# Low halves of weights by accumulating DMAs in more stages, additions on VectorE, and reordered heads, in a two-block transformer kernel

## The chip, the cores and the metric

The kernel runs as one program on one core of a Trainium2 chip. The metric is the device time of one execution in microseconds (us). Before the change three executions took 1567.94, 1572.04 and 1572.07 us, median 1572.04. The execution that was profiled took 1570.88 us, of which the trace covers a span of 1569.1 us.

Names of engines: PE is TensorE (PEld its weight load), DVE is VectorE, ACT is ScalarE, POOL is GpSimd, SP issues plain DMAs. "L174" is line 174 of the kernel before.

## The reference

512 tokens of width 1024 pass through two blocks, all in float32. Cut to what matters:

```python
def first_block(x, mem, ...):                       # one layer
    h = rmsnorm(x, g_mix_pre)
    aq, ak, av, iq, ik, iw, bq, bk, bv, cq, gate_logits = split(h @ w_in)
    mkv = rmsnorm(mem, g_mem) @ w_mem_kv
    ya = dsa_attention(aq, ak, av, iq, ik, iw, rel_bias) @ w_up_a   # top-k keys by an index score
    yb = stick_breaking_attention(bq, bk, bv) @ w_up_b
    yc = memory_attention(cq, mk, mv) @ w_up_c
    merged = gates[0] * ya + gates[1] * yb + gates[2] * yc
    x = x + rmsnorm(merged @ w_out, g_mix_post)
    gu = rmsnorm(x, g_ffn_pre) @ w_ffn_in
    x = x + rmsnorm((silu(gu[:F]) * gu[F:]) @ w_ffn_out, g_ffn_post)

def second_block(x, p, ...):
    h = h + mlstm_layer(h)       # conv + silu on q, k; gates i, f; per head: decay matrix, values, norm, o, z
    h = ple_add(h, p[0])         # h + (p @ w_proj) * sigmoid(rms_norm(h) @ w_gate)
    k, v = shared_kv(h)          # rotary keys
    h = h + dilated_layer(h, k, v)   # three dilations, softmax over them, silu(z) gate, w_out
    h = ple_add(h, p[1])

# stick breaking, per head, with z = q k^T / 8 and a strictly causal mask:
log_beta = log_sigmoid(z)
tail = reverse_cumsum(log_sigmoid(-z)) - log_sigmoid(-z)
a = exp(log_beta + tail);  out = a @ v
```

## The kernel before, in words

**Every product is three products.** TensorE multiplies values rounded to a short float32 form, so both operands are kept as a rounded high half and a low half that holds the rest, and a product is high·high + low·high + high·low. A block of weights of 128 x 1024 (512 KB) gives 24 matmuls of 512 columns, called a unit below.

**Weights are prepared just ahead of their use.** `pre` (L150) takes the next block in the order of use: SP loads it into one of two buffers `wraw`, the high half `wh` is a rounded copy (one of three buffers), the low half `wl` (one of three) is made in one of three ways. Either DVE subtracts `wraw - wh` (L174), or POOL does (L172), or, where `low_dma` is set, ACT writes `-wraw` rounded into `wl` and a DMA issued by POOL adds the same block from memory on top (L165, L166). `pool_share` chooses between L172 and L174; `low_dma` holds in the stick-breaking stage alone, where `hi_dve` also lets DVE make the high half (L160) instead of ACT (L162). Blocks scaled by a gain ("quad" and "fmg", in the dilated layer and elsewhere) go through `split` and are in none of these ways. A block is prepared as soon as a buffer comes free.

**Stages in order of the span (us):** index projections 0 to 55, memory scores and memory attention to 150, stick-breaking attention to 350, sparse attention ("dsa") to 510, up-projections and w_out to 585, first post-norm to 617, FFN to 963, second post-norm with the first projection of the mLSTM to 1004, gates ("mg") and the other q and k projections to 1039, v (token-major, two groups) and o to 1126, mLSTM heads to 1218, w_out_a to 1256, first ple 1257 to 1307, dilated layer to 1511, second ple to 1564.

**The order of work** is the order in which the code is written, with generators: a branch `yield`s after some units, and `weave` takes turns between two such generators (heads and projections that fill in between). Each engine runs its own instructions in that order, and so does POOL's queue, which issues the DMAs of L166.

**Parts that the steps below touch.** `post_norm` (L460) makes, per 128 rows of features, `t` (L469, DVE), `h + t` (DVE for the first, POOL for the others, L471 and L473), `xh` and `xl` (the split for the next stage) and the sum of squares `ss` (L304). Branch results are added to `merged` by POOL (L519). A stick-breaking head (L806) collects `z` in one PSUM buffer; ACT takes |z| (L821) and a copy of z (L823); the chain of exp, ln, max-and-add (L826), scan (L827) and subtraction (L828) then works on the copy. An mLSTM head has a broadcast `Mb` of the running maximum over partitions on POOL (L1186), a product `dg` with the identity (L1190), a broadcast `eb` (L1201), and at its end `norm` (L1235 and after). A POOL broadcast and a POOL tensor operation belong to different code libraries: the program has an instruction "ISA" without operands wherever the one follows the other. At the end of the dilated layer, `logits`, `z_tile`, `values` and `finish` run per head, and `w_out_b_2` follows.

Of the kernel before, what the change touches and what calls it, by code (L numbers as in the profile page):

```python
# [88 lines left out]
class K:  # L89
    def __init__(s, ctx, tc, A, dbg=None):  # L90
        s.ctx, s.tc, s.nc, s.A = ctx, tc, tc.nc, A
        s.dbg = dbg
        s.order = []
        s.since, s.fence, s.fenced = [], None, False
        s.ready, s.share, s.pool_share, s.hi_dve, s.low_dma = {}, 0.0, 0.0, False, False
        s.b4 = None
# [39 lines left out]
    def pre(s, *spec):  # L136

        nc = s.nc
        u = len(s.order)
        s.order.append(spec)  # L140
        raw = s.wraw.tile([128, 1024], F32, name="wraw")
        for c in ((0, 512), (512, 1024)) if u == 0 else ((0, 1024),):
            nc.sync.dma_start(raw[:, c[0]:c[1]], s.A["W"][u][:, c[0]:c[1]])
        hi = s.whp.tile([128, 1024], F32R, name="wh")
        lo = s.wlp.tile([128, 1024], F32R, name="wl")
        if u == 0:
            for c in (slice(0, 512), slice(512, 1024)):
                s.split(hi[:, c], lo[:, c], raw[:, c])
            s.ready[spec] = hi, lo
            return  # L150
        if spec[0] in ("quad", "fmg"):

            n = 2 if spec[0] == "quad" else 8
            for i in range(n):
                c = slice(1024 // n * i, 1024 // n * (i + 1))
                s.split(hi[:, c], lo[:, c], raw[:, c], s.vec(spec[-1], spec[3] * n + i))
            s.ready[spec] = hi, lo
            return
        if s.hi_dve:
            nc.vector.tensor_copy(hi, raw)  # L160
        else:
            nc.scalar.activation(hi, raw, AF.Copy)  # L162
        if s.low_dma:

            nc.scalar.activation(lo, raw, AF.Copy, scale=-1.0)  # L165
            nc.gpsimd.dma_start(lo, s.A["W"][u], accum_op=OP.add)  # L166
            s.ready[spec] = hi, lo
            return
        s.share += s.pool_share
        if s.share >= 1.0:  # L170
            s.share -= 1.0
            nc.gpsimd.tensor_tensor(lo, raw, hi.bitcast(F32), op=OP.subtract)  # L172
        else:
            nc.vector.tensor_tensor(lo, raw, hi.bitcast(F32), op=OP.subtract)  # L174
        s.ready[spec] = hi, lo
# [285 lines left out]
    def post_norm(s, r, S, g, gn):  # L461

        nc = s.nc
        s.mark("postnorm")
        bc, _ = s.rstd_from(S[0], T, 1024, cols=False)
        s.S = [None]
        for k in range(8):
            t = s.tmp.tile([128, T], F32, name="t512")
            nc.vector.scalar_tensor_tensor(t, r[:, k], s.vec(g, k), bc, op0=OP.mult, op1=OP.mult)  # L469
            if k < 1:  # L470
                nc.vector.tensor_tensor(s.h[:, k], s.h[:, k], t, op=OP.add)  # L471
            else:
                nc.gpsimd.tensor_tensor(s.h[:, k], s.h[:, k], t, op=OP.add)  # L473
            s.split(s.xs[0][:, k], s.xs[1][:, k], s.h[:, k], s.vec(gn, k))
            s.ssq_add(s.S, s.h[:, k])
# [17 lines left out]
    def up_g(s, wname, yh, yl, G, first):  # L493
# [15 lines left out]
        for j in range(4):  # L509
            for mm in range(2):  # L510
                m = 2 * j + mm
                prods(m, (3,) if m < 3 else range(4))
                ps = pss[m]
                if first:
                    nc.vector.tensor_tensor(s.merged[:, m], ps, G[:, m], op=OP.mult)
                else:
                    t = s.tmp.tile([128, T], F32, name="t512")
                    nc.vector.tensor_tensor(t, ps, G[:, m], op=OP.mult)
                    nc.gpsimd.tensor_tensor(s.merged[:, m], s.merged[:, m], t, op=OP.add)  # L519
                yield  # L520
# [39 lines left out]
    def dsa_mem(s, x, iqc):  # L560
# [5 lines left out]
        with ExitStack() as br:  # L566
# [10 lines left out]
            with ExitStack() as c:  # L577
# [15 lines left out]
                s.fm4("w_in", iqc, s.xs, ev, mid=mid)  # L593
                s.pool_share = 0.5
                ikh = one.tile([128, T], F32R, name="ikh")
# [168 lines left out]
    def stick_branch(s, br):  # L764
        nc = s.nc
        s.mark("stick")
        s.pool_share, s.hi_dve, s.low_dma = 1.0, True, True
        vp = s.pool("bv", 1, ctx=br)
# [37 lines left out]
        def logits(h):  # L806
# [14 lines left out]
            nc.scalar.activation(e, z, AF.Abs)  # L821
            c = wk.tile([128, 1280], F32, name="e")
            nc.scalar.activation(c, z, AF.Copy)  # L823
            s.act(e, e, AF.Exp, scale=-1.0)
            s.act(e, e, AF.Ln, bias=1.0)
            nc.vector.scalar_tensor_tensor(e, c, 0.0, e, op0=OP.max, op1=OP.add)  # L826
            nc.vector.tensor_tensor_scan(e[:, ::-1], keep, e[:, ::-1], 0.0, op0=OP.mult, op1=OP.add)  # L827
            nc.vector.tensor_tensor(c, c, e, op=OP.subtract)  # L828
            s.act(c, c, AF.Exp)
            st[h] = c  # L830

# [76 lines left out]
    def dsa_branch(s, br):  # L908

        nc, A = s.nc, s.A  # L910
        s.mark("dsa")
        s.pool_share, s.hi_dve, s.low_dma = 0.5, False, False
        vp = s.pool("av", 1, ctx=br)
# [103 lines left out]
        s.drain(ua[0])  # L1017
        s.pool_share = 0.0

# [69 lines left out]
    def mlstm(s):  # L1089
# [3 lines left out]
        with ExitStack() as ph:  # L1093
# [3 lines left out]
            def mid():  # L1097
                yield
                yield
                yield  # L1100
                st["bc"], st["cols"] = yield from s.rstd_g(s.S[0], T, 1024)
                s.S = [None]
# [7 lines left out]
            with ExitStack() as c3:  # L1110
# [5 lines left out]
                def conv(m, ps):  # L1116
# [3 lines left out]
                    for t in range(1, 4):  # L1120
                        nc.vector.scalar_tensor_tensor(qk[:, m], c[:, 1 + t:1 + t + T], s.vec("conv", 8 * t + m),
                                                       qk[:, m], op0=OP.mult, op1=OP.add)
                s.pool_share = 1.0
                s.fm4("w_in_a_2", [128 * m for m in range(4)], xs, conv, mid=mid)
                bc, cols = st["bc"], st["cols"]
                gp = s.pool("mg", 1, ctx=c3)
# [3 lines left out]
                def ev(ps):  # L1130
# [14 lines left out]
                    nc.vector.tensor_scalar(nM, nM, -1.0, None, op0=OP.mult)  # L1145
                s.fm(("mg",), xs, ev, m=64)
                for m in range(4, 8):
# [6 lines left out]
                for m in range(8):  # L1154
                    s.act(qk[:, m], qk[:, m], AF.Silu)
            s.pool_share = 0.0
            o = qp.tile([128, 8, T], F32, name="o")
# [16 lines left out]
            with ExitStack() as c2:  # L1174
# [83 lines left out]
                def main():  # L1258
# [4 lines left out]
                    for h in range(3):  # L1263
                        values(h)
                        weights(h + 1)
                        if h < 2:
                            decay(h + 2)
                        yield 2
                        norm(h)
                        yield 2  # L1270
                    values(3)
# [48 lines left out]
    def ple(s, l):  # L1320
        nc, A = s.nc, s.A
        s.mark("ple%d" % l)
        with ExitStack() as ph:
            pp = s.pool("ple", 1, ctx=ph)
            wk = s.pool("plew", 3, ctx=ph)
            pw = pp.tile([128, 8, T], F32, name="pw")
            nc.sync.dma_start(pw, s.pw[l])
            xs = (pp.tile([128, 8, T], F32R, name="xh"), pp.tile([128, 8, T], F32R, name="xl"))
            ks = range(8)
# [37 lines left out]
    def dilated(s):  # L1367
        nc, A = s.nc, s.A
        s.mark("dil")
        xs = s.xs  # L1370
        s.pool_share = 0.0
        with ExitStack() as ph:
# [105 lines left out]

            def keys():
                for h in range(4):  # L1480
# [6 lines left out]
            def queries(X, tiles):  # L1487
                for j, (h, g) in enumerate(tiles):
                    if g == 0:
# [113 lines left out]
            XK = rope(pk, ck)  # L1603
            X0 = qquad(0, {5: [keys]})
            X1 = qquad(1, {5: [lambda: queries(X0, QS[0])]})
            logits(0)
            z_tile(0)
            pv = quad("w_kv_2", [512 + 128 * h for h in range(4)], "norm_kv", {5: [lambda: queries(X1, QS[1])]}, False)
            for t in range(4):
                nc.scalar.activation(v[:, t], pv[t], AF.Copy, scale=cols[:, t:t + 1])  # L1610

                for c in range(4):
                    nc.sync.dma_start(vq[32 * t:32 * t + 32, c, :], v[c:128:4, t, :])
            logits(1)
            z_tile(1)
            X2 = qquad(2, {4: [lambda: values(0)]})
            z_tile(2)
            values(1)
            z_tile(3)
            for h in range(2):  # L1620
                finish(h)
            queries(X2, QS[2])
            logits(2)
            out = s.fm4_g("w_out_b_2", [128 * m for m in range(4)], xs, ev, ks=range(4))
            prods(4, range(2))
            logits(3)
            next(out)
            next(out)
            values(2)
# [11 lines left out]
            s.b4 = None  # L1641
            s.pool_share = 1.0
        if s.dbg: s.dbg("h3", s.h)
# [118 lines left out]
```

## Time and profile before

| what | value |
|---|---|
| median of three executions | 1572.04 us (1567.94 to 1572.07) |
| the profiled execution | 1570.88 us |
| its span | 1569.1 us, 17934 instructions |
| PE busy | 1511.0 us (96%), 6813 instructions |
| DVE busy | 981.8 us (63%), 1421 instructions |
| ACT busy | 721.4 us (46%), 1194 instructions |
| POOL busy | 263.5 us (17%), 165 instructions |
| mean granted clock of TensorE | 0.983 of full speed |
| low halves by DVE, by POOL, by DMA | 149, 40, 26 |

The page of the profile has the busy time of each engine, the span in 40 slices, the DMA queues, the chain of work that ended last, and the costliest groups of instructions. Other views answer for a stretch of time: what each engine waited for, the busy time in a list of windows with the granted clock, and a timeline of instructions. "Idle before <- X" is the time that an engine stood idle before an instruction and what released it; "issue" there means that nothing the trace shows was waited for.

### The profile page before, as it was taken

Reading aid. Unit: us, or ns where it says so; the run is one execution under the profiler, and the core shown is the slowest. Engines: PE = TensorE matmul, PEld = TensorE weight load, DVE = VectorE, ACT = ScalarE, POOL = GpSimd, SP = SyncE. Lnnn points to the kernel's source line nnn. Section 1 sums busy time; section 2 is a strip of 40 time slices with the busy share of each in tenths; the row PEclk is TensorE's granted clock in tenths of the full one; section 3 lists DMA queues with packets and bytes.
Section 4 is the critical chain, followed back from the end, with each engine's and each line's share of the span. In section 5 each row is a group of like instructions: output and inputs, shape, how many; then the busy total and the mean of one; then the engine's idle time right before and its main releaser. Section 6 shows DMA issues by size and latency. Waiting matters only on the chain.

```text
span 1569.1 us, 17934 instructions
## 1 busy us (share of the span) xinstructions
PE 1511.0 (96%) x6813; PEld 1237.2 (79%) x6813; DVE 981.8 (63%) x1421; ACT 721.4 (46%) x1194; POOL 263.5 (17%) x165
## 2 busy tenths in 40 slices
PE   8999999999999999999999999899999999999988
PEld 6787877778777877888888887688877778989766
DVE  6899867664776638443234335773367566886966
ACT  5544356663455446332222324353465354654543
POOL 3211110113311404110011102610022000010022
PEclk9999999999999999999999999999999999999989
DMA  5332875552222533332233333223211333223222
GB/s 191 107 102 70 176 159 133 118 131 95 91 78 74 161 105 125 101 95 94 94 96 103 97 94 127 75 81 119 83 54 55 93 135 108 81 79 96 67 93 95
DMA packets 48806, 162.01 MB, mean 103 GB/s; under 512 B 5712, under 2 KB 7120, under 8 KB 48464
## 3 DMA queue, kind: packets, MB, share of 16 engines
q1 hardware_dynamic: 44976, 147.24, 29.8%
q0 software_dynamic: 3744, 13.63, 4.9%
q8 instruction: 53, 0.87, 0.2%
q14 instruction: 33, 0.27, 0.1%
HBM read 153.50 MB, written 6.29 MB: 102 GB/s over the span
## 4 chain that ended last, share of the span: by engine, by line
PE 69%; DVE 18%; ACT 8%; issue 4%; POOL 1%; DMA 1%; SPq 0%; ACTq 0%; DVEq 0%; POOLq 0%
PE dps L128 45%; PE b L128 18%; PE z L128 3%; ACT e L122 2%; DVE ss L304 2%; DVE xl L256 1%; DVE e L827 1%; PE aps L128 1%; DVE wl L174 1%; ACT wh L162 1%; DVE aTl L253 1%; DVE score L747 1%; PE o L128 1%; DVE e L693 1%; DVE e L828 1%
## 5 line engine op out<-in xcount | busy, mean ns | idle before, releaser
L128 PE MATMUL dps<-xh,wh 128*128 128x512 f32 (+2 forms) x996 | 396.4, 398 | 5.3 <-DVE aTl L253 4.2
L162 ACT ACTIVATE wh<-wraw 128x1024 fp32r<-128x1024 f32 x189 | 199.9, 1058 | 413.3 <-PE dps L128 258.8
L128 PE MATMUL dps<-xh,wl 128*128 128x512 f32 (+2 forms) x996 | 388.3, 390 | 0.2 <-DMA wl<-in_W 0.2
L128 PE MATMUL dps<-xl,wh 128*128 128x512 f32 (+2 forms) x996 | 388.1, 390 | 0.0
L174 DVE TENSOR_TENSOR wl<-wraw,wh 128x1024 fp32r<-128x1024 f32 x149 | 188.2, 1264 | 168.9 <-ACT wh L162 163.9
L128 PEld LDWEIGHTS dps<-xh,wh 128*128 128x128 f32 (+1 forms) x996 | 187.4, 188 | 51.5 <-DVE aTl L253 6.2
L128 PEld LDWEIGHTS dps<-xh,wl 128*128 128x128 f32 (+1 forms) x996 | 187.1, 188 | 41.1 <-DMA wl<-in_W 0.7
L128 PEld LDWEIGHTS dps<-xl,wh 128*128 128x128 f32 (+1 forms) x996 | 187.5, 188 | 40.2 <-issue 1.8
L172 POOL TENSOR_TENSOR wl<-wraw,wh 128x1024 fp32r<-128x1024 f32 x40 | 102.5, 2563 | 319.8 <-ACT wh L162 295.9
L128 PE MATMUL b<-wh,xh 128*128 128x512 f32 x288 | 115.4, 401 | 0.0
L128 PE MATMUL b<-wl,xh 128*128 128x512 f32 x288 | 114.1, 396 | 0.0
L128 PE MATMUL b<-wh,xl 128*128 128x512 f32 x288 | 113.9, 396 | 0.0
L128 PE MATMUL b<-xh,wh 128*128 128x512 f32 x208 | 87.0, 418 | 7.0 <-ACT xh L252 3.9
L128 PE MATMUL b<-xl,wh 128*128 128x512 f32 x208 | 85.7, 412 | 8.3 <-DVE xl L256 7.4
L128 PE MATMUL b<-xh,wl 128*128 128x512 f32 x208 | 85.0, 409 | 3.3 <-DVE wl L174 1.8
L1044 POOL TENSOR_TENSOR g<-g,bc 128x512 f32<-128x512 f32 x22 | 38.9, 1767 | 246.8 <-ACT g L122 246.8
L128 PEld LDWEIGHTS b<-wh,xh 128*128 128x128 f32 x288 | 69.8, 242 | 7.0 <-issue 0.2
L128 PEld LDWEIGHTS b<-wl,xh 128*128 128x128 f32 x288 | 69.8, 242 | 6.6
L128 PEld LDWEIGHTS b<-wh,xl 128*128 128x128 f32 x288 | 69.7, 242 | 6.6
L128 PE MATMUL dps<-fh,wh 128*128 128x512 f32 x176 | 69.3, 394 | 0.0
L128 PE MATMUL dps<-fl,wh 128*128 128x512 f32 x176 | 69.3, 394 | 0.0
L128 PE MATMUL dps<-fh,wl 128*128 128x512 f32 x176 | 69.3, 394 | 0.0
(360 smaller groups left out, 2609.9 us busy)
## 6 DMA issues: line engine op xcount, KB each, us to landing
wraw<-in_W SPq DMA_DIRECT2D x239, 512.0 KB, 3.6
wl<-in_W POOLq DMA_DIRECT2D x26, 512.0 KB, 7.1
h<-in_x SPq DMA_DIRECT2D x16, 256.0 KB, 4.0
pw<-pwo SPq DMA_DIRECT2D x16, 256.0 KB, 2.0
pw<-pw SPq DMA_DIRECT2D x2, 2048.0 KB, 7.8
strip<-in_relb SPq DMA_DIRECT2D x8, 256.0 KB, 2.6
out<-h SPq DMA_DIRECT2D x7, 256.0 KB, 2.0
G<-in_mem SPq DMA_DIRECT2D x1, 1024.0 KB, 9.1
```

The source lines that it names most:

```text
L122: i = s.nc.scalar.activation(out, in_, func, **kw)
L128: s.nc.tensor.matmul(out, l, r, start=start, stop=stop, skip_group_check=True)
L162: nc.scalar.activation(hi, raw, AF.Copy)
L172: nc.gpsimd.tensor_tensor(lo, raw, hi.bitcast(F32), op=OP.subtract)
L174: nc.vector.tensor_tensor(lo, raw, hi.bitcast(F32), op=OP.subtract)
L253: nc.vector.tensor_tensor(lo, src, hi.bitcast(F32), op=OP.subtract)
L256: nc.vector.scalar_tensor_tensor(lo, src, scale, hi.bitcast(F32), op0=OP.mult, op1=OP.subtract)
L304: nc.vector.tensor_tensor(S[0], S[0], t, op=OP.add)
L693: nc.vector.tensor_scalar(e[:, t], e[:, t], rs[:, t:t + 1], None, op0=OP.mult)
L747: nc.vector.match_replace(w, m8, w, SENT)
L827: nc.vector.tensor_tensor_scan(e[:, ::-1], keep, e[:, ::-1], 0.0, op0=OP.mult, op1=OP.add)
L1044: nc.gpsimd.tensor_tensor(g, g, st["bc"], op=OP.mult)
```

## The change

1. **Low halves.** The subtraction on POOL (L172) is gone, and `dma_share` replaces `pool_share` and `low_dma`: where it is 1, ACT writes `-wraw` and POOL issues the accumulating DMA; where it is 0, DVE subtracts. It is 1 from the index projections on through the memory, stick-breaking and sparse stages and the up-projections that stand in them, in the mLSTM from its first projection to its end, in the first ple, from `logits(2)` of the dilated layer to the end of the kernel. The FFN, w_out and the rest of the dilated layer have 0.
2. **Additions.** The additions of L473 and L519 go from POOL to DVE.
3. **Stick breaking.** No copy of z: L826 and L828 read z in PSUM.
4. **mLSTM start.** The reciprocal norm is taken four half units into the first projection instead of three, and the gate projection's first half comes before its transposes.
5. **mLSTM heads.** The weave takes a turn between `values(h)` and `weights(h + 1)`, and one less after `norm(h)`.
6. **ple.** The tiles of the stage are placed in another order in memory, for the first ple with a gap between them.
7. **Dilated layer.** Keys and queries are turned in two halves on two hooks (5 and 6); the third query projection runs before the values' projection; at the end `logits(2)`, `values(0)`, `logits(3)`, `values(1)` come earlier, and `values(2)` and `values(3)` stand together ahead of `finish(2)` and `finish(3)`.

In counts: ACT writes 134 negative copies in place of 26 and drops 8 copies of z; POOL issues 134 accumulating DMAs in place of 26 and loses 40 subtractions and 30 additions; DVE makes 81 low halves in place of 149 and gains 30 additions. PE's instructions are as many as before.

```diff
@@ pre
-        if s.low_dma:
+        s.share += s.dma_share
+        if s.share >= 1.0:
+            s.share -= 1.0
             nc.scalar.activation(lo, raw, AF.Copy, scale=-1.0)
             nc.gpsimd.dma_start(lo, s.A["W"][u], accum_op=OP.add)
-            s.ready[spec] = hi, lo
-            return
-        s.share += s.pool_share
-        if s.share >= 1.0:
-            s.share -= 1.0
-            nc.gpsimd.tensor_tensor(lo, raw, hi.bitcast(F32), op=OP.subtract)
         else:
             nc.vector.tensor_tensor(lo, raw, hi.bitcast(F32), op=OP.subtract)
@@ post_norm
-            if k < 1:
-                nc.vector.tensor_tensor(s.h[:, k], s.h[:, k], t, op=OP.add)
-            else:
-                nc.gpsimd.tensor_tensor(s.h[:, k], s.h[:, k], t, op=OP.add)
+            nc.vector.tensor_tensor(s.h[:, k], s.h[:, k], t, op=OP.add)
@@ branch results
-                    nc.gpsimd.tensor_tensor(s.merged[:, m], s.merged[:, m], t, op=OP.add)
+                    nc.vector.tensor_tensor(s.merged[:, m], s.merged[:, m], t, op=OP.add)
@@ index, stick, dsa
-                s.pool_share = 0.5
+                s.dma_share = 1.0
...
-        s.pool_share, s.hi_dve, s.low_dma = 1.0, True, True
+        s.dma_share, s.hi_dve = 1.0, True
...
-        s.pool_share, s.hi_dve, s.low_dma = 0.5, False, False
+        s.dma_share, s.hi_dve = 1.0, False
@@ stick-breaking head
-            c = wk.tile([128, 1280], F32, name="e")
-            nc.scalar.activation(c, z, AF.Copy)
             s.act(e, e, AF.Exp, scale=-1.0)
             s.act(e, e, AF.Ln, bias=1.0)
-            nc.vector.scalar_tensor_tensor(e, c, 0.0, e, op0=OP.max, op1=OP.add)
+            nc.vector.scalar_tensor_tensor(e, z, 0.0, e, op0=OP.max, op1=OP.add)
             nc.vector.tensor_tensor_scan(e[:, ::-1], keep, e[:, ::-1], 0.0, op0=OP.mult, op1=OP.add)
-            nc.vector.tensor_tensor(c, c, e, op=OP.subtract)
-            s.act(c, c, AF.Exp)
-            st[h] = c
+            nc.vector.tensor_tensor(e, z, e, op=OP.subtract)
+            s.act(e, e, AF.Exp)
+            st[h] = e
@@ mLSTM start
-                yield
-                yield
-                yield
+                for _ in range(4):
+                    yield
...
-                s.pool_share = 1.0
-                s.fm4("w_in_a_2", [128 * m for m in range(4)], xs, conv, mid=mid)
-                bc, cols = st["bc"], st["cols"]
+                s.dma_share = 1.0
+                first = s.fm4_g("w_in_a_2", [128 * m for m in range(4)], xs, conv, mid=mid)
+                for _ in range(8):
+                    next(first)
...
-                s.fm(("mg",), xs, ev, m=64)
+                second = s.fm_g(("mg",), xs, ev, m=64)
+                next(second)
+                s.drain(first)
+                bc, cols = st["bc"], st["cols"]
+                s.drain(second)
...
-            s.pool_share = 0.0
@@ mLSTM heads
                         values(h)
+                        yield 1
                         weights(h + 1)
...
                         norm(h)
-                        yield 2
+                        yield 1
@@ dilated layer, end
-            pv = quad("w_kv_2", [512 + 128 * h for h in range(4)], "norm_kv", {5: [lambda: queries(X1, QS[1])]}, False)
+            X2 = qquad(2, {5: [lambda: queries(X1, QS[1], (0, 1))], 6: [lambda: queries(X1, QS[1], (2, 3))]})
+            logits(1)
+            z_tile(1)
+            pv = quad("w_kv_2", [512 + 128 * h for h in range(4)], "norm_kv", {5: [lambda: queries(X2, QS[2], (0, 1))], 6: [lambda: queries(X2, QS[2], (2, 3))]}, False)
...
-            logits(1)
-            z_tile(1)
-            X2 = qquad(2, {4: [lambda: values(0)]})
+            s.dma_share = 1.0
+            logits(2)
             z_tile(2)
+            values(0)
+            logits(3)
             values(1)
             z_tile(3)
             for h in range(2):
                 finish(h)
-            queries(X2, QS[2])
-            logits(2)
             out = s.fm4_g("w_out_b_2", [128 * m for m in range(4)], xs, ev, ks=range(4))
-            prods(4, range(2))
-            logits(3)
             next(out)
             next(out)
+            prods(4, range(2))
             values(2)
+            values(3)
             finish(2)
+            finish(3)
             next(out)
-            values(3)
-            finish(3)
```

Three places show how instructions stand in a row now.

POOL's queue in the mLSTM between the last low halves of the q and k projections and the second head's broadcasts, before:

```order
L172 TENSOR_TENSOR wl<-wraw,wh 128x1024 x3
L1186 ISA
L1186 ISA Mb<-row 128x512
L1190 ISA
L1190 TENSOR_TENSOR dg<-Mb,csts 128x512
L1201 ISA
L1201 ISA eb<-row 128x512
L1186 ISA Mb<-row 128x512
L1201 ISA eb<-row 128x512
```

and after:

```order
L168 DMA wl<-in_W 128x1024 x7
L1180 ISA
L1180 ISA Mb<-row 128x512
L168 DMA wl<-in_W 128x1024
L1184 ISA
L1184 TENSOR_TENSOR dg<-Mb,csts 128x512
L1195 ISA
L1195 ISA eb<-row 128x512
L168 DMA wl<-in_W 128x1024
L1180 ISA Mb<-row 128x512
L1195 ISA eb<-row 128x512
L168 DMA wl<-in_W 128x1024 x13
```

Before, no weight work stands between the broadcasts; now one accumulating DMA stands between `Mb` and `dg` (it is the low half of the first o unit) and one behind `eb` (the first unit of the second v group), each behind an "ISA" that changes the library.

DVE in the third stick-breaking head's turn, before:

```order
L826 SCALAR_TENSOR_TENSOR e<-e 128x1280
L253 TENSOR_TENSOR aTl<-dps,aTh 128x512
L253 TENSOR_TENSOR aTl<-dps,aTh 128x256
L253 TENSOR_TENSOR aTl<-aps,aTh 128x512
L827 SCALAR_TENSOR_TENSOR e<-keep,e 128x1280
L160 CAST wh<-wraw 128x1024
L796 SCALAR_TENSOR_TENSOR t_2272<-dps,bc 128x512
L828 TENSOR_TENSOR e<-e 128x1280
```

and after:

```order
L817 SCALAR_TENSOR_TENSOR e<-z,e 128x1280
L249 TENSOR_TENSOR aTl<-dps,aTh 128x512
L818 SCALAR_TENSOR_TENSOR e<-keep,e 128x1280
L249 TENSOR_TENSOR aTl<-dps,aTh 128x256
L249 TENSOR_TENSOR aTl<-aps,aTh 128x512
L819 TENSOR_TENSOR e<-z,e 128x1280
L160 CAST wh<-wraw 128x1024
```

The scan and the subtraction have moved up between the `aTl` of the head before, and the chain's first and last steps read z.

ACT at the end of the dilated layer (l: logits of a head, t from dps and aps: a head's `finish`, xh from kT: its rounded result, ss from h: the sum of squares after w_out), before:

```order
L122 ACTIVATE l<-l 128x896
L122 ACTIVATE l<-l 128x1024
L252 ACTIVATE xh<-kT 128x512
L1575 ACTIVATE t_11398<-dps 128x4x128
L122 ACTIVATE t_11401<-aps 128x512
L122 ACTIVATE t_11401<-t_11401 128x512
L252 ACTIVATE xh<-kT 128x512
L300 ACTIVATE ss<-h 128x512
```

and after:

```order
L122 ACTIVATE l<-l 128x896
L122 ACTIVATE l<-l 128x1024
L1574 ACTIVATE t_11441<-dps 128x4x128
L122 ACTIVATE t_11444<-aps 128x512
L122 ACTIVATE t_11444<-t_11444 128x512
L1574 ACTIVATE t_11460<-dps 128x4x128
L248 ACTIVATE xh<-kT 128x512
L122 ACTIVATE t_11463<-aps 128x512
L122 ACTIVATE t_11463<-t_11463 128x512
L248 ACTIVATE xh<-kT 128x512
L296 ACTIVATE ss<-h 128x512
```

The two heads' `values` follow one another now, and the first `xh` stands behind the second head's start.

## Rows read from the trace of the kernel before

**Rows 1.** Waits of TensorE, whole run: line waited for, us, times, longest.

```profile
PE b L128 <- DVE xl L256: 7.4, 6, 2.2
PE aps L128 <- DVE ss L304: 5.3, 5, 2.2
PE aps L128 <- DVE t L1235: 4.8, 2, 2.6
PE dps L128 <- DVE aTl L253: 4.2, 3, 1.8
PE b L128 <- ACT xh L252: 3.9, 1, 3.9
PE dps L128 <- DVE e L253: 3.0, 1, 3.0
PE dps L128 <- DVE t L518: 2.0, 1, 2.0
PE dps L1476 <- DVE kT L1483: 1.9, 1, 1.9
...
PE dps L128 <- DVE a L1554: 1.8, 1, 1.8
```

**Rows 2.** Windows: busy us of each engine, granted clock, DMA share.

```profile
141.00:151.00 10.00, 6.38 (x16) 4.53 (x16) 8.86 (x20) 3.76 (x6) 0.00 (x0) 0.66 0.33 105
154.00:205.00 51.00, 51.00 (x230) 42.08 (x229) 41.20 (x82) 17.97 (x23) 9.20 (x14) 1.00 0.85 182
966.00:1004.00 38.00, 30.31 (x126) 22.78 (x125) 34.84 (x25) 19.64 (x30) 26.87 (x16) 1.00 0.39 127
1005.02:1010.28 5.26, 5.26 (x13) 4.00 (x14) 0.16 (x1) 0.18 (x1) 1.03 (x1) 0.50 0.08 30
1484.00:1499.20 15.20, 7.38 (x22) 4.35 (x21) 12.32 (x17) 5.59 (x7) 2.08 (x1) 0.66 0.12 34
```

**Rows 3.** Chain of waits from 1055 to 1070: start us, us, what.

```profile
1060.90 5.44 PE dps L128 x24
```

**Rows 4.** Costliest groups of the page: count, busy us, mean ns.

```profile
L162 ACT ACTIVATE wh<-wraw 128x1024 fp32r<-128x1024 f32 x189 | 199.9, 1058 | 413.3 <-PE dps L128 258.8
...
L174 DVE TENSOR_TENSOR wl<-wraw,wh 128x1024 fp32r<-128x1024 f32 x149 | 188.2, 1264 | 168.9 <-ACT wh L162 163.9
...
L172 POOL TENSOR_TENSOR wl<-wraw,wh 128x1024 fp32r<-128x1024 f32 x40 | 102.5, 2563 | 319.8 <-ACT wh L162 295.9
```

**Rows 5.** DMA, 154 to 205 us: share of queues; KB, us to landing.

```profile
q0 software_dynamic: 1224, 4.49, 48.5%
q1 hardware_dynamic: 1296, 4.72, 35.9%
...
wl<-in_W POOLq DMA_DIRECT2D x9, 512.0 KB, 7.5
wraw<-in_W SPq DMA_DIRECT2D x8, 512.0 KB, 4.9
```

**Rows 6.** VectorE by shape, 966 to 1000 us: busy us, mean ns.

```profile
L304 DVE TENSOR_TENSOR ss<-ss,t 128x512 f32<-128x512 f32 x7 | 14.2, 2033 | 0.7 <-ACT t L303 0.7
...
L471 DVE TENSOR_TENSOR h<-h,t 128x512 f32<-128x512 f32 x1 | 0.7, 681 | 0.0
```

**Rows 7.** Timeline of POOL, 1045 to 1066 us: start, us, what, idle before.

```profile
1048.60 0.80 POOL L1186 PARTITION_BROADCAST Mb<-row  x1 [21.37 <-DMA row<-M]
1056.13 1.28 POOL L1190 TENSOR_TENSOR dg<-Mb,csts 128x512 f32<-128x512 f32 x1 [6.73 <-issue]
1063.53 0.80 POOL L1201 PARTITION_BROADCAST eb<-row  x1 [6.12 <-issue]
```

**Rows 8.** Timeline of all engines, 222 to 238 us, one stick-breaking head.

```profile
223.31 1.23 ACT L823 ACTIVATE e<-z 128x1280 f32<-128x1280 f32 x1
...
235.95 0.44 PE L128 MATMUL z<-H,S 128*128 128x512 f32 x1
236.00 1.48 DVE L828 TENSOR_TENSOR e<-e 128x1280 f32<-128x1280 f32 x1
```

More of the change, by code (lines that the diff above doesn't have):

```diff
@@ L94, in __init__ @@
         s.since, s.fence, s.fenced = [], None, False
-        s.ready, s.share, s.pool_share, s.hi_dve, s.low_dma = {}, 0.0, 0.0, False, False
+        s.ready, s.share, s.dma_share, s.hi_dve = {}, 0.0, 0.0, False
         s.b4 = None
@@ L1017, in dsa_branch @@
         s.drain(ua[0])
-        s.pool_share = 0.0
+        s.dma_share = 0.0
     def ffn(s):
@@ L1155, in mlstm @@
                     s.act(qk[:, m], qk[:, m], AF.Silu)
-            s.pool_share = 0.0
             o = qp.tile([128, 8, T], F32, name="o")
@@ L1325, in ple @@
             wk = s.pool("plew", 3, ctx=ph)
+            xh = pp.tile([128, 8, T], F32R, name="xh")
             pw = pp.tile([128, 8, T], F32, name="pw")
+            if l == 0:
+                pp.tile([128, 8, T], F32, name="gap")
+            xs = xh, pp.tile([128, 8, T], F32R, name="xl")
             nc.sync.dma_start(pw, s.pw[l])
-            xs = (pp.tile([128, 8, T], F32R, name="xh"), pp.tile([128, 8, T], F32R, name="xl"))
             ks = range(8)
@@ L1370, in dilated @@
         xs = s.xs
-        s.pool_share = 0.0
+        s.dma_share = 0.0
         with ExitStack() as ph:
@@ L1477, in turned, with keys @@
                 return ps
-            def keys():
-                for h in range(4):
+            def keys(hs):
+                for h in hs:
                     ps = turned(XK, h)
@@ L1485, in dilated, with queries @@
             qt = {}
-            def queries(X, tiles):
-                for j, (h, g) in enumerate(tiles):
+            def queries(X, tiles, js):
+                for j in js:
+                    h, g = tiles[j]
                     if g == 0:
@@ L1603, in dilated @@
             XK = rope(pk, ck)
-            X0 = qquad(0, {5: [keys]})
-            X1 = qquad(1, {5: [lambda: queries(X0, QS[0])]})
+            X0 = qquad(0, {5: [lambda: keys((0, 1))], 6: [lambda: keys((2, 3))]})
+            X1 = qquad(1, {5: [lambda: queries(X0, QS[0], (0, 1))], 6: [lambda: queries(X0, QS[0], (2, 3))]})
             logits(0)
             z_tile(0)
-            pv = quad("w_kv_2", [512 + 128 * h for h in range(4)], "norm_kv", {5: [lambda: queries(X1, QS[1])]}, False)
+            X2 = qquad(2, {5: [lambda: queries(X1, QS[1], (0, 1))], 6: [lambda: queries(X1, QS[1], (2, 3))]})
+            logits(1)
+            z_tile(1)
+            pv = quad("w_kv_2", [512 + 128 * h for h in range(4)], "norm_kv", {5: [lambda: queries(X2, QS[2], (0, 1))], 6: [lambda: queries(X2, QS[2], (2, 3))]}, False)
             for t in range(4):
@@ L1641, in dilated @@
             s.b4 = None
-            s.pool_share = 1.0
+            s.dma_share = 1.0
         if s.dbg: s.dbg("h3", s.h)
```

## Prediction

> **What bounds the kernel now.** I read the waits of TensorE over the whole run first, because a kernel can only get shorter here where PE stops waiting, or where its clock rises. The largest lines name DVE: xl 7.4, ss 5.3, t L1235 4.8, aTl 4.2, e 3.0, t L518 2.0, kT 1.9, a 1.8; ACT's xh has 3.9 [rows 1]. They sum to 34.3 us, the pool of what can be won from waits. Then the windows by stage: from 154 to 205 PE is busy for 51.00 of 51.00 us at clock 1.00; from 966 to 1004 for 30.31 of 38.00, with DVE at 34.84 and POOL at 26.87; at 141 to 151 and 1484 to 1499.2 for 6.38 of 10.00 and 7.38 of 15.20, at a mean clock of 0.66 [rows 2]. So PE bounds the kernel, and DVE bounds it at the borders between stages. [...] In 1005.02 to 1010.28 a half unit took 5.26 us [rows 2]; a whole one at full clock takes 5.44 [rows 3], so the half should have taken 2.72, and 2.5 us went to the clock.
>
> **Cost of the parts.** DVE makes 149 low halves at 1.264 us, POOL 40 at 2.563; ACT copies a block in 1.058 [rows 4]. The change takes 68 x 1.264 = 86 us from DVE, and POOL's 102.5. ACT gains 108 copies, 108 x 1.06 = 114 us, less 8 x 1.23 [rows 8]. The 30 additions cost DVE between 0.68 alone and 2.03 (what a two-input operation on DVE takes in the mean while POOL works beside it, ss) [rows 6]; I take 0.7, 21 us, because POOL's tensor work that stands beside them goes too. Beside busy PE all of this is free; what counts is the border where it ends last.
>
> *Memory attention's end (141 to 151).* 16 matmuls stand in 10.00 us; at 0.227 (5.44/24) they need 3.6. DVE, busy for 8.86, loses its low halves here, but top-k steps stand in their place. +3 (0 to 6). *Index stage:* DVE loses some low halves, the first accumulating DMAs may land late: +1 (-1 to 3).
>
> *Sparse attention:* t L518 2.0 and part of aTl's 4.2 [rows 1] come where POOL's subtraction stretches a DVE operation; both go. +3.5 (1 to 5). *First post-norm:* one of xl's waits (longest 2.2) and part of its half clock: +2.5 (1 to 4).
>
> *Second post-norm and mLSTM start.* 38.00 - 30.31 = 7.7 us idle and 2.5 of clock [rows 2]. DVE's work per 128 rows becomes t, addition, xl, ss, four operations of some 0.7 us, 2.8 x 8 = 23 us in place of 34.84. But ACT now copies each block twice there beside xh and the squares. +8 (4 to 10).
>
> *mLSTM heads:* t L1235 4.8 in two waits [rows 1]. The new turn gives the first one more PE work ahead; the second hangs on POOL's chain of broadcasts. With the clock behind them: +3.5 (1 to 6).
>
> *Dilated layer:* halved hooks remove kT's 1.9 and some of q's: +2.5 (1 to 3). At its end a 1.8, xh 3.9 [rows 1] and the rest of 15.20 - 7.38 = 7.8, with some 10 us at half clock (mean 0.66), in half of which PE works, worth 2.7: 10.5 in all. The two heads' values in a row leave one chain uncovered, some 3: +8 (3 to 10).
>
> *mLSTM v and o: a new wait.* POOL's queue is in order, and it now carries the low halves. In the row after `Mb` at 1048.60 `dg` starts at 1056.13 with 6.73 us idle that nothing else explains ("issue"), and `eb` at 1063.53 with 6.12 [rows 7]: a change of library each. Nobody waited, as no weight hung on POOL there. Now o's first low half is behind `Mb`, and that of the second v group behind `eb`. The library change ahead of `Mb`, hidden in 21.37 us of idle time before, now starts behind the fourth v unit's DMA, about 1047.5 (its buffer is free at 1060.90 - 3 x 5.44 = 1044.6, then two copies of 1.06 and the issue). With 6.5 for it and 0.80, `Mb` ends near 1055; o's DMA is issued at 1056 and lands 6 to 7 us later, 1062.5, 1.5 late. Then 6.73 + 1.28 + 6.12 + 0.80 = 14.9: the next DMA is issued near 1071 and lands near 1078 (7.5 from issue [rows 5]). PE wants it at 1060.90 + 5.44 + 1.5 = 1068: 10 us late. With 2.5 of clock and 1 for the units behind: -15. If POOL sent DMAs on past a library change it would be about -1; if a third broadcast falls in, -20.
>
> *Stick breaking.* PE starts the next z at 235.95, while the subtraction of the head before runs to 236.00 + 1.48 = 237.48 [rows 8]. It now reads z itself, so z is free 1.5 later than PE comes, less the 1.23 of the dropped copy: about 0.3 a head, some heads more, and each wait shifts what follows: -1 (-6 to +3).
>
> *First unit(s) behind a border:* the ples' first low halves come by DMA behind ACT's xh copies and beside the stage's other loads: -2.5 (-6 to +1). *Units in general:* with three buffers a unit may take 2 x 5.44 = 10.9 us from free buffer to use; two copies (2.1) and 7.5 make 9.6, so 1.3 is left. -1.5 (-6 to 0).
>
> Sum: 3 + 1 + 3.5 + 2.5 + 8 + 3.5 + 2.5 + 8 - 15 - 1 - 2.5 - 1.5 = +12. The profiled execution took 1570.88 with a span of 1569.1, 1.2 below the median 1572.04; I forecast 1570.9 - 12 = 1559.
>
> **Rivals.** *A. The library change holds nothing up* (issues go past it, or the DMAs have slack): the -15 becomes -1, 1545. For it: the trace has no POOL DMA near a library change. Against: the `eb` behind `dg` waits for nothing else and still starts 6.12 late.
>
> *B. The waits only move.* ACT takes 114 us more and becomes what ends last at the borders: half of the +32 comes back, 1575, or somewhat less, 1570. For it: at 966 to 1004 ACT has 19.64 of 38.00 before, with 8 or 9 more copies 29, packed into 30. Against: DVE and POOL each had more.
>
> *C. Slower: accumulating DMAs land late in every unit.* Its place is all 108 new units; the price is what a landing exceeds the slack by. The 26 before land 7.5 after issue, with the plain loads and theirs at 48.5 + 35.9% of the DMA engines' time [rows 5], and PE did not wait in that stretch [rows 2]. There DVE made the high halves beside ACT's negative copy; now ACT makes both, in a row. It decides from a landing of 8.8 us: at 9.0 it is 0.2 x 108 = 22 us, so 1559 + 22 = 1581. [...]
>
> **Numbers.** The forecast 0.46 (own range 1551 to 1567); A 0.20 (1538 to 1551); B 0.20 (1565 to 1576); C 0.14 (1574 to 1595). 0.3%, about what a measurement of this kernel tells from no change, is 4.7 us. Faster (under 1567.3): 0.45 + 0.20 + 0.06 = 0.71; same: 0.01 + 0.13 + 0.02 = 0.16; slower 0.01 + 0.12 = 0.13. The range to hold 8 of 10 reaches half into A and through most of B: 1545 to 1575.
>
> **What the profile after would show.** Right: PE's lines for xl, ss, t L518 and xh are near nothing; 966 to 1004 is a stretch of some 30 us; one new line, PE waiting for the DMA of wl, of 10 us or more at the first unit of the second v group, with half clock behind it, and POOL's `dg` and `eb` still 6 to 7 us late. Wrong: no such line (A); ACT's wh or wl ending the waits at the borders (B); many small waits for wl by DMA in all stages (C), or one for z's PSUM in the stick-breaking heads. Most of all the forecast fails if the order in POOL's queue costs less or more than one library change per instruction.

## The result and the profile after

The changed kernel took 1588.62 us (median of four executions, 1582.07 to 1589.66) against 1571.93 before: a ratio of 1.0103, 95% interval 1.0085 to 1.0121. It is slower by about 16.7 us; the forecast was 1559, 13 faster. The profiled execution is the lowest of the four, 1582.07, with a span of 1580.3; every reading of the trace below is of that one.

First TensorE's waits over the whole run, after, in the columns of [rows 1]:

```profile
PE b L128 <- DMA wl<-in_W: 24.3, 7, 12.7
PE aps L128 <- DVE t L1229: 8.5, 1, 8.5
PE dps L128 <- DMA wl<-in_W: 5.2, 5, 1.5
PE z L128 <- DVE e L819: 4.1, 4, 1.3
PE b L128 <- DVE wl L170: 3.9, 3, 1.9
PE dps L128 <- ACT pwo L1310: 3.1, 2, 2.7
...
PE b L128 <- DVE xl L249: 2.7, 2, 2.3
PE b L128 <- ACT xh L248: 2.2, 2, 1.5
...
PE b L128 <- DVE xl L252: 0.8, 2, 0.5
...
PE dps L128 <- DVE aTl L249: 0.5, 1, 0.5
```

The lines of [rows 1] that were to go have gone or are small: xl of the norms 7.4 to 0.8, aTl 4.2 to 0.5, kT, a, e and t L518 without a line, xh 3.9 to 2.2. In their place stand 29.5 us of waits for low halves by DMA, a norm's wait of 8.5 in place of 4.8 in two, and new ones for z (e L819) and for ACT (pwo).

The windows, after, at the places of [rows 2] and at the two longest waits:

```profile
138.00:148.00 10.00, 10.00 (x49) 8.33 (x48) 9.76 (x26) 9.48 (x13) 1.73 (x2) 1.00 0.58 113
152.00:203.00 51.00, 51.00 (x230) 42.00 (x228) 37.47 (x71) 17.90 (x22) 8.35 (x13) 1.00 0.87 187
963.00:1001.00 38.00, 33.48 (x133) 25.04 (x132) 20.95 (x32) 24.63 (x37) 5.89 (x9) 0.96 0.80 204
1061.00:1079.10 18.10, 5.43 (x15) 4.01 (x14) 0.69 (x1) 2.52 (x3) 4.98 (x6) 0.62 0.37 71
1184.50:1198.60 14.10, 5.57 (x13) 3.51 (x12) 5.87 (x7) 6.64 (x12) 4.69 (x4) 0.64 0.03 10
...
1521.00:1533.00 12.00, 5.27 (x13) 4.13 (x13) 9.65 (x16) 10.41 (x16) 2.57 (x3) 0.72 0.87 198
```

The end of the memory attention is without a gap now, and in the second post-norm DVE is busy for 20.95 us in place of 34.84 [rows 2]. In the fourth to sixth window PE works for 5.4, 5.6 and 5.3 us of 18.1, 14.1 and 12.0, at a mean clock of 0.62 to 0.72. The trace has the granted clock at 0.50, called half clock below, for 13.65 us from 1065.40 on, 10.24 from 1188.28 on and 6.83 from 1526.20 on; PE's waits there ended at 1074.50, 1193.31 and 1527.75, so it worked at half clock for 4.6, 5.2 and 5.3 us behind them.

Where the matmul of the same number stands in each trace (us from the start; both have 6813; within the dilated layer the order of work differs, so 6460 is not the same matmul in both):

| matmul no., place | before | after | difference | added in the stretch |
|---|---|---|---|---|
| 510, memory logits | 112.7 | 116.7 | +4.0 | +4.0 |
| 680, stick-breaking v | 153.6 | 151.0 | -2.6 | -6.6 |
| 1360, stick-breaking heads | 302.1 | 302.2 | +0.1 | +2.7 |
| 2550, w_out | 559.0 | 558.8 | -0.2 | -0.3 |
| 4250, FFN's end | 953.7 | 951.1 | -2.6 | -2.4 |
| 4590, first v group | 1042.8 | 1035.0 | -7.8 | -5.2 |
| 4760, second v group | 1081.4 | 1091.7 | +10.3 | +18.1 |
| 5440, w_out_a | 1239.4 | 1253.2 | +13.8 | +3.5 |
| 6460, dilated end | 1475.5 | 1483.2 | +7.7 | -6.1 |
| 6800, last unit | 1562.6 | 1573.8 | +11.2 | +3.5 |

The 18.1 us stand at the place that the prediction named. POOL's timeline, after, against [rows 7]:

```profile
1047.49 0.80 POOL L1180 PARTITION_BROADCAST Mb<-row  x1 [8.71 <-DMA row<-M]
1048.14 1.11 POOL L168 DMA_DIRECT2D wl<-in_W  x1
1059.07 1.28 POOL L1184 TENSOR_TENSOR dg<-Mb,csts 128x512 f32<-128x512 f32 x1 [9.81 <-issue]
1066.69 0.80 POOL L1195 PARTITION_BROADCAST eb<-row  x1 [6.34 <-issue]
1067.34 1.11 POOL L168 DMA_DIRECT2D wl<-in_W  x1
```

`dg` and `eb` are late by 9.81 and 6.34 us of "issue", and the next low half's DMA is issued at 1067.34, 19 us after the one before it. What is called a change of library here is in the trace as POOL's instruction MODIFY_POOL_CONFIG, at 1048.98 and at 1060.55; POOL does no other work from there to `dg` and to `eb`, which start 10.1 and 6.1 us after it. TensorE's timeline shows who waited:

```profile
1074.50 0.79 PE L128 MATMUL b<-wl,xh 128*128 128x512 f32 x1 [12.67 <-DMA wl<-in_W]
```

The same queue delays the fourth head's decay matrix. POOL's timeline some 100 us later:

```profile
1169.01 0.87 POOL L168 DMA_DIRECT2D wl<-in_W  x1 [3.54 <-ACT wl L167]
1177.60 0.80 POOL L1195 PARTITION_BROADCAST eb<-row  x1 [7.72 <-DVE o L1226]
1178.25 1.11 POOL L168 DMA_DIRECT2D wl<-in_W  x1
1181.77 0.80 POOL L1180 PARTITION_BROADCAST Mb<-row  x1 [2.41 <-DMA row<-M]
1189.46 1.25 POOL L1184 TENSOR_TENSOR dg<-Mb,csts 128x512 f32<-128x512 f32 x1 [6.89 <-issue]
```

A DMA for which ACT's copy came late (3.54) starts at 1169.01, then come a library change (at 1169.84), `eb`, another DMA, `Mb`, another change (6.89) and `dg` at 1189.46. What held `eb` is not settled by its row: the profile names DVE's `o`, which ended 0.3 us before, but 7.8 us from the change to `eb` is also no more than the other changes took here (6.1 to 10.1). ACT's queue shows what follows:

```profile
1190.74 1.28 ACT L122 ACTIVATE E<-dg,uc 128x128 f32<-128x128 f32 x4 [5.27 <-POOL dg L1184]
1191.92 0.61 ACT L1228 ACTIVATE t<-o 128x512 f32<-128x512 f32 x1
```

The four exponentials of the fourth head wait 5.27 us for `dg`, and the square `t` for the second head's norm stands right behind them. PE waited for it until 1193.31, the 8.5 us of t L1229 in the first list:

```profile
1193.31 2.07 PE L128 MATMUL aps<-t,csts 128*128 128x512 f32 x2 [8.53 <-DVE t L1229]
```

### The profile page after: what moved, and what is told of

It reads as the page before. It is cut to its first block, busy times and chain, and to the rows that moved or that the text cites. A ratio compares the mean times of both kernels' runs of the same rounds, so it can differ in the third digit from the quotient of the medians.

```text
span 1580.3 us, 18130 instructions
## 1 busy us (share of the span) xinstructions
PE 1506.0 (95%) x6813; PEld 1231.9 (78%) x6813; DVE 851.0 (54%) x1383; ACT 811.8 (51%) x1294; POOL 205.9 (13%) x203
## 4 chain that ended last, share of the span: by engine, by line
PE 66%; issue 18%; DMA 6%; DVE 3%; ACT 3%; POOL 3%; SPq 0%; POOLq 0%; ACTq 0%; DVEq 0%
PE dps L128 46%; PE b L128 15%; DMA wl<-in_W 4%; PE z L128 3%; POOL wl L168 2%; PE aps L128 1%; DMA pw<-pwo 1%; ACT wh L162 1%; ACT wl L167 1%; PE o L128 1%; DMA row<-M 1%; ACT E L122 1%; PE dps L1474 0%; DMA h<-in_x 0%; DVE xl L252 0%
## 5 line engine op out<-in xcount | busy, mean ns | idle before, releaser
L168 POOL DMA_DIRECT2D wl<-in_W x134 | 118.4, 885 | 768.0 <-ACT wl L167 740.1
L167 ACT ACTIVATE wl<-wraw 128x1024 fp32r<-128x1024 f32 x134 | 140.5, 1048 | 81.1 <-PE dps L128 40.3
L170 DVE TENSOR_TENSOR wl<-wraw,wh 128x1024 fp32r<-128x1024 f32 x81 | 100.8, 1244 | 104.2 <-ACT wh L162 104.1
```

## The experiments

Two theories at first. *L:* changes of POOL's library hold up the low halves queued behind them. *D:* accumulating DMAs are late everywhere, whatever else POOL does. "Before" in each run's ratio is the kernel before on the same chip.

**e1: the mLSTM's low halves by DVE again.**

```diff
                     s.act(qk[:, m], qk[:, m], AF.Silu)
+            s.dma_share = 0.0
             o = qp.tile([128, 8, T], F32, name="o")
...
+            s.dma_share = 1.0        # behind w_out_a
```

> The changed kernel, but from the mLSTM's v projection to the end of w_out_a DVE makes the low halves again (no accumulating DMA there). Theory L (changes of POOL's library hold up the low halves queued behind them): the waits of 2.79 and 12.67 us for wl by DMA at the v groups go with most of their half clock (13.65 us at 0.50, some 6 us), and of the 8.53 us ahead of the second head's norm about half: 25 us less than the changed kernel's 1588.6, 1560 to 1568. Rival D (accumulating DMAs are late everywhere, whatever else POOL does): this undoes about a third of the new ones, so about a third of the loss beyond the gains: 1578 to 1584.

Measured: 1566.25 (1562.87 to 1576.87, ten executions), ratio 0.9974 [0.9957, 0.9991]. As L says, 22 us less than the changed kernel.

**e2: the DMAs kept, the library changes taken away.**

```diff
-                    nc.gpsimd.tensor_tensor(dg, Mb.rearrange(...), ...)
+                    nc.vector.tensor_tensor(dg, Mb.rearrange(...), ...)
...
-                        nc.gpsimd.tensor_tensor(o[:, m], o[:, m], z[m], op=OP.mult)
+                        nc.vector.tensor_tensor(o[:, m], o[:, m], z[m], op=OP.mult)
```

> The changed kernel with every accumulating DMA kept, but the additions dg and the products of o with z in the mLSTM heads made by DVE instead of POOL (12 operations of some 0.7 us), so that POOL's queue has only broadcasts and DMAs there and one library change in place of seven. Theory L: the same waits go as without the DMAs, 1560 to 1568. Rival D: nothing but the 12 operations changes, 1583 to 1590.

Measured: 1561.56 (1556.77 to 1568.45), ratio 0.9937 [0.9915, 0.9959]: 27 us less than the changed kernel with every DMA in place. POOL's timeline of this run at the same place:

```profile
1048.95 0.80 POOL L1180 PARTITION_BROADCAST Mb<-row  x1 [8.24 <-ACT wh L162]
1049.60 1.11 POOL L168 DMA_DIRECT2D wl<-in_W  x1
1051.46 0.79 POOL L1195 PARTITION_BROADCAST eb<-row  x1 [0.74 <-DMA row<-en]
1052.31 0.88 POOL L168 DMA_DIRECT2D wl<-in_W  x1
```

`Mb`, a DMA, `eb` and the next DMA start within 3.4 us, where the changed kernel took 20; the t L1229 line is gone from PE's waits. Together with e1 this settles L for these two places: the DMAs are late there because of what POOL does between them. (The edit takes POOL's 12 tensor operations away together with the changes; those took some 1.3 us each, so the gaps of 6 to 10 us that the changes bring are the larger part.)

**e3: that part alone on the kernel before.**

```diff
             s.pool_share = 0.0
+            s.low_dma = True
             o = qp.tile([128, 8, T], F32, name="o")
...
+            s.low_dma = False        # behind w_out_a
```

> The kernel before with one part of the change alone: from the mLSTM's v projection to the end of w_out_a the low halves come by accumulating DMA. Theory L: the waits of the changed kernel at the v groups (15 us and 6 of half clock) and at the second head's norm (4 to 5) come to the kernel before: 1572 + 20 to 28 = 1592 to 1600. Rival D: a third of the new DMAs, 1574 to 1582. If the changed order of the heads is what made the norm's wait longer: 1590 to 1594 without that wait.

Measured: 1595.35 (1593.44 to 1597.78), ratio 1.0155 [1.0140, 1.0170], 23.6 us more. Its waits of PE:

```profile
PE aps L128 <- DVE t L1236: 10.6, 2, 10.0
PE dps L128 <- DMA wl<-in_W: 10.2, 2, 8.8
...
PE b L128 <- DMA wl<-in_W: 4.3, 2, 3.9
```

The norm's wait (10.0 the longest) comes with the old order of the heads too, so the new order did not make it.

**e4: the second ple's first four units by DVE.**

```diff
+            if l:
+                s.dma_share = 0.0
             s.fm4("w_ple_gate_2", ...)
+            s.dma_share = 1.0
```

> The changed kernel with the four units of the second ple's first product made by DVE. Theory: PE waits 6.73 us there only because the first unit's low half lands some 6.6 us after ACT's copies, which stand behind the xh copies; DVE takes 1.24: the wait falls to 1 to 2 us and most of the 6.83 us of half clock goes, 8 us less: 1578 to 1583. Rival (the queue of xh copies on ACT is what is late): the wait goes to DVE's wl or to xl and 1585 to 1590 is left.

Measured: 1578.99 (1578.20 to 1582.73), 9.6 us less than the changed kernel. In the changed kernel's trace PE waits for the landing of this DMA, which nothing held up once it was issued:

```profile
1521.14 6.57 DMA wl<-in_W
...
1527.75 0.79 PE L128 MATMUL b<-xh,wl 128*128 128x512 f32 x1 [6.73 <-DMA wl<-in_W]
```

In e4 a wait of 2.4 us for DVE's low half takes its place, the longest of this line:

```profile
PE b L128 <- DVE wl L170: 5.7, 4, 2.4
```

**e5: e2 and e4 together** (both diffs above).

> Both edits together on the changed kernel: dg and the products of o with z on DVE, and the four units of the second ple's first product by DVE. If the two waits are separate causes their gains add: 1561.6 - 9.6 = 1552 (1548 to 1556). If the second ple's wait only paid because the clock was already down, less: 1556 to 1561.

Measured: 1554.57 (1553.48 to 1555.26), ratio 0.9891 [0.9873, 0.9910]. Of the 9.6 us of e4, 7.0 are left on top of e2: nearly additive. What is left of waits for low halves by DMA:

```profile
PE dps L128 <- DMA wl<-in_W: 6.7, 5, 2.5
...
PE b L128 <- DMA wl<-in_W: 4.4, 4, 3.0
```

**e6: e5 with ACT's copy of z restored** (the change's part 3 undone).

> The kernel with both edits, and ACT's copy of z in the stick-breaking heads restored as in the kernel before. Theory S (reading z in PSUM holds its buffer until the subtraction, and the waits of PE for it, 1.1 to 1.3 us in some heads, are followed by half clock in some executions): those waits go, 3 to 8 us less than without the copy and a narrower spread. Rival (the kernel before had waits of the same size there for aTl, and eight copies of 1.23 us load ACT): within 2 us either way, or up to 4 more.

Measured: 1552.41 (1547.58 to 1554.37), 2 us less with overlapping spreads: undecided. In place of z's waits (4.1) stand those for aTl (4.2).

**e7: e5 with the index and memory stages' low halves by DVE.**

```diff
                 s.fm4("w_in", iqc, s.xs, ev, mid=mid)
-                s.dma_share = 1.0
```

> The kernel with both edits, and the low halves of the index and memory stages (up to stick breaking) made by DVE in place of DMA. Theory (the first accumulating DMAs land late at the index stage, waits of 0.8 to 2.2 us): 2 to 4 us less. Rival (DVE was what ended last at the end of the memory attention, where the changed kernel gained 6.7 us): that gain is lost and the sum is 2 to 5 us more.

Measured: 1549.06 (1542.60 to 1550.18), 5.5 us less. The rival falls: DVE carries these low halves and the memory attention's end keeps its gain (6.7 us between matmuls 510 and 680, as in the changed kernel).

**e8: the kernel before without POOL's tensor work.**

```diff
-            nc.gpsimd.tensor_tensor(lo, raw, hi.bitcast(F32), op=OP.subtract)
+            nc.vector.tensor_tensor(lo, raw, hi.bitcast(F32), op=OP.subtract)
...            # and the additions of L473 and L519 likewise
```

> The kernel before with POOL's 40 low halves and 30 additions made by DVE, nothing else changed. Theory P (POOL's tensor work stretches DVE's operations at the borders between stages, 2.03 us for a sum of squares in place of 0.7): the waits at the post-norms, at sparse attention and at the second ple shrink, 6 to 12 us less than 1571.8: 1560 to 1566. Rival (it was DVE's amount of work that ended last): 40 x 1.26 + 30 x 0.7 = 71 us more on DVE, 1572 to 1582.

Measured: 1547.85 (1547.12 to 1549.10), ratio 0.9850 [0.9831, 0.9868]: 23 us less than before, double what the theory expected, although DVE has 70 operations more. DVE by shape at the second post-norm in this run, against [rows 6]:

```profile
L256 DVE SCALAR_TENSOR_TENSOR xl<-h,vecs,xh 128x512 fp32r<-128x512 f32 x8 | 5.9, 743 | 0.0
...
L304 DVE TENSOR_TENSOR ss<-ss,t 128x512 f32<-128x512 f32 x8 | 5.5, 682 | 0.0
L473 DVE TENSOR_TENSOR h<-h,t 128x512 f32<-128x512 f32 x7 | 4.8, 681 | 0.0
```

The sum of squares takes 0.682 us in place of 2.033. DVE's busy time over the run falls from 981.8 to 970.9 us with 70 operations more: POOL's work had cost DVE more than it saved.

**e9: the changed kernel without its new DMAs** (dma_share 1 in stick breaking alone).

> The changed kernel without any of its new accumulating DMAs: they stay in the stick-breaking stage as before, and DVE makes all other low halves; additions on DVE, reordered heads and dilated end as in the change. Theory M (what gained is the end of POOL's tensor work and the new orders; what lost is the new DMAs): the kernel before without POOL's tensor work, 1547.9, less the first of the two norm waits (1.9 and some clock) and 6 at the dilated layer: 1537 to 1543. Rival (the new order of the heads itself makes the second norm's wait of 8.5 us): 1546 to 1552.

Measured: 1548.79 (1543.96 to 1553.33), ratio 0.9854 [0.9825, 0.9884]: 40 us less than the changed kernel, but no better than e8: the changes 3 to 7 together gave nothing here. The traces of e8 and e9, counted by weight loads, of which each trace has all 6813, show where gains and losses cancel. From number 5440 on (first ple, dilated layer, second ple) e9 gains 8 us on e8, and it gives them back in stick breaking (4.7, part 3), at the mLSTM's start (3.3) and in its heads (2.1).

**e10: e9 with e2's edit.**

> The same with dg and the products of o with z on DVE, so that POOL changes its library once in the mLSTM. If the second norm's wait of 2.3 us hangs on POOL's library changes even without DMAs: 2 to 4 us less than the run without this edit. If DVE's 12 more operations end later there: 0 to 3 more.

Measured: 1541.15 (1535.35 to 1543.39), ratio 0.9801 [0.9772, 0.9829]: 7.6 less, more than expected; even without DMAs in the queue the library changes had been on the path of the heads (eb L1242 3.8 and t L1227 1.7 us in e9's waits of PE, both gone in e10). Between matmuls 4760 and 5440, the heads and w_out_a, e9 is 0.2 us shorter than before and e10 8.5.

**e11: e8 with the additions left on POOL.**

> The kernel before with POOL's 40 low halves by DVE, its 30 additions left on POOL. If each of POOL's tensor operations stretches DVE alike, two thirds of the 24 us that both together gained (102.5 of some 152 us of POOL's work): 1553 to 1558. If the additions are the ones that matter, as they stand between t and xl of the same rows: 1562 to 1568. If they are harmless: 1548.

Measured: 1551.10 (1549.95 to 1553.09), ratio 0.9871 [0.9850, 0.9892], 20 of the 23 us: the low halves on POOL were most of the harm. The additions have the other 3, which is rough: e8 and e11 ran on two chips, whose medians of the kernel before differ by 2.4.

**e12: e10 with ACT's copy of z.**

> The kernel without new DMAs and without library changes, with ACT's copy of z in stick breaking restored. In the earlier pair the copy was worth 2 us with overlapping spreads (1552.4 against 1554.6). If that is real, 1 to 4 us less than without it; if the waits for aTl that come in place of those for z cost as much, within 1.5 us.

Measured: 1537.26 (1536.75 to 1537.91), ratio 0.9781 [0.9758, 0.9805], 3.9 us less in the median and within 1.2 us from run to run. As e10's own lowest, 1535.35, lies below that, the times alone leave the copy's worth undecided. In the two traces stick breaking (matmuls 680 to 1360) is 6.5 us shorter with the copy, and e10's has 13.7 us of half clock there, e12's none; but e10's profiled execution is the slowest of its four. By the median e12 is the fastest version: the additions and the orders of the change and DVE's low halves, with no new DMA, no library changes in the heads and no reading of z in PSUM. The line of busy engines on its page, and below it that of the changed kernel:

```profile
PE 1498.8 (98%) x6805; PEld 1231.2 (80%) x6813; DVE 974.2 (63%) x1503; ACT 722.1 (47%) x1194; POOL 99.4 (6%) x83
```

```profile
PE 1506.0 (95%) x6813; PEld 1231.9 (78%) x6813; DVE 851.0 (54%) x1383; ACT 811.8 (51%) x1294; POOL 205.9 (13%) x203
```

## Why the prediction was wrong

**Where the miss lies.** The forecast's terms against the stretches of the table, in us of time (plus is slower):

| stretch (matmul no.) | terms of the forecast | forecast | measured |
|---|---|---|---|
| start to 510 | index stage | -1 | +4.0 |
| 510 to 680 | memory attention's end | -3 | -6.6 |
| 680 to 1360 | stick breaking | +1 | +2.7 |
| 1360 to 4250 | sparse attention, first post-norm | -6 | -2.7 |
| 4250 to 4590 | second post-norm, mLSTM start | -8 | -5.2 |
| 4590 to 4760 | the new wait | +15 | +18.1 |
| 4760 to 5440 | mLSTM heads | -3.5 | +3.5 |
| 5440 to the end | dilated layer, first units | -8 | -2.6 |
| everywhere | units in general | +1.5 | in the rows above |

The sums are -12 and +11.2, 23.2 apart. The other 6.5 us of the miss is that the profiled execution is the lowest of its four.

**Right: the mechanism of the largest loss.** "A new wait" in the mLSTM's v and o, at the first unit of the second v group, behind `dg` and `eb`: forecast 10 us and 15 in all, measured 12.67 and +18.1 in the stretch. Rival A falls by [rows 7] and the POOL rows after alike. Part of the closeness is luck: `Mb` came at 1047.49 (forecast near 1055), the gap ahead of `dg` was 9.81 us and not 6.73, and PE came at 1061.8 and not at 1068, as the whole stage began 7.8 us earlier.

**Wrong, step "mLSTM heads: +3.5", the largest error.** It followed PE and the chain of broadcasts, and priced neither the new DMAs in the same queue nor the library changes that stay in the heads. In place of a gain of 3.5 the stretch lost 3.5. The second norm waited 8.5 us, with 10.24 us of half clock from 1188.28 on, 5.2 of it behind the wait. In e9, without the DMAs, the new order gained 0.2 there. Without the library changes the stretch is 8.5 us shorter than before, with the DMAs (e2) and without (e10). So the changes, with the 12 operations of POOL that go with them in these runs, cost 8 us in the heads by themselves, and the DMAs behind them some 4 more.

**Wrong, step "Index stage: +1" (-1 to 3).** The stage lost 4.0 where 1 was to be won; with DVE's low halves it gains 3.9 to 4.4 (traces of e7 and e9). e7 has 5.5 us for it in the median. What was too small in it is the price of the DMAs and of their copies on ACT: up to 160 us PE waits 3.6 us for low halves by DMA and 3.6 for ACT's `r` in e5's trace, and for neither in e7's.

**Mis-sized, step "First unit(s) behind a border: -2.5" (-6 to +1).** At the second ple the price was a landing's 6.57 us with nothing in front of it, as ACT copies this unit behind xh: 6.73 of wait and 5.3 us of half clock behind it (to 1533.03), 9.6 by e4. At the first ple PE waited 0.7 for it.

**Mis-sized, "Units in general: -1.5".** e5 and e10 differ by all the other new DMAs: 13.4 us, of which e7 finds 5.5 in the index and memory stages. That is rival C in kind, but not in its place: e5's list has nine waits for wl by DMA, 11.1 us in all and up to 3.0 each, not 0.2 us in each of 108 units. That they follow bursts on ACT was not tested. *Sparse attention: +3.5* fits this: between matmuls 1360 and 2550 the changed kernel gains 0.3, and e9, without DMAs there, 3.3.

**Right, "Cost of the parts", but for another kernel.** The gains at the borders, 18 us forecast from memory attention to mLSTM start, are real: e8 has 23 for the end of POOL's tensor work, and its trace is 24.7 ahead at matmul 4590. But they needed no DMA, and the changed kernel is only 7.8 ahead there. +3 and +2.5 came as 6.6 and 2.4, and +8 at the second post-norm as 5.2, with a new wait for ACT's `pwo` (3.1) that e9 and e10, without the DMAs and their copies on ACT, do not have; this part of rival B is true. *Dilated layer:* 10.5 forecast, 6.1 measured between matmuls 5440 and 6460 (the first ple included); why it is less was not tried. *Stick breaking: -1*: 2.7 in the stretch; z's waits replace those for aTl at 4.1 against 4.2.

**Landing times.** They did not decide here: the accumulating DMAs landed 7.5 us after issue in the median over the whole changed run, as in [rows 5], under the 8.8 from which rival C counts; at the longest wait, 12.67 us, it was the issue that was late, 19 us after the one before it.

**What stays open.** The changed kernel's executions differ by 7 us, those before by 4. The four mean clocks lie between 0.981 and 0.986. An estimate from these: 0.004 less over 1585 us is some 13 us more of half clock, which would cost 6. So the spread may be that waits are followed by half clock in some executions and not in others, but one execution of each kernel was traced, so this is not shown; in the fifteen executions of the kernel before that stand beside e1 to e4, the fastest (1568.69) had 0.987 and the slowest (1572.98) 0.988. What each of parts 4 to 7 is worth alone was not tried either: e12 is 10.6 us below e8 (on another chip), with e2's edit in it, which e9 and e10 put at 7.6.

## What to carry to other kernels

Work moved to an engine's queue stands behind everything in that queue, as the second v group's low half did here behind `dg` and `eb`, late by 9.81 and 6.34 us: list what is queued between two items that must be on time, library changes included, before a transfer is moved there. When a helper engine slows the main one, try first to give the work back to the main one; here that alone was worth 23 us, while the changed kernel with its new DMAs was 40 us slower than without them. A transfer that is hidden in a steady stream (PE busy for 51.00 of 51.00 us from 152 to 203) can cost its full latency at the first unit behind a border (a landing of 6.57 us at the second ple, and 6.73 of wait).

## What the runs showed of the hardware

**POOL beside DVE.** In this kernel POOL's tensor operations cost DVE more than the work they took from it: with POOL's 40 low halves (2.563 us each) given to DVE the kernel was 20 us faster (e11), and with the additions too DVE's sum of squares took 0.68 in place of 2.03 us (e8). In the trace before, twelve sums of squares began while a tensor operation of POOL ran and took longer than alone (1.53 to 2.90 us in place of 0.68), and each of them ended 0.55 us after POOL's, whether that was a short one (1.73) or a long one (2.86):

```profile
981.22 2.86 POOL L172 TENSOR_TENSOR wl<-wraw,wh 128x1024 fp32r<-128x1024 f32 x1
981.73 2.90 DVE L304 TENSOR_TENSOR ss<-ss,t 128x512 f32<-128x512 f32 x1
...
989.86 1.74 POOL L473 TENSOR_TENSOR h<-h,t 128x512 f32<-128x512 f32 x1 [1.29 <-DVE t L469]
990.37 1.77 DVE L304 TENSOR_TENSOR ss<-ss,t 128x512 f32<-128x512 f32 x1
```

A thirteenth, at 1524.04, began under a subtraction of POOL that took 3.46 us, and took 0.68 as alone. Why DVE's operation ends with POOL's in the twelve was not shown.

**Library changes.** In the changed kernel `dg` and `eb` start 9.81 and 6.34 us late behind a change of POOL's library, and the DMA behind `eb` with them: it is issued at 1067.34, 19 us after the DMA before it. In e2, without a change between them, the same DMA is issued 2.7 us after the one before it (1049.60 and 1052.31).
